# Other layouts for two DRAM scratch tensors, other places for an attention head's loads, and an own staging tile for the new frames' result

## The chip, the cores and the metric

The program runs on one core of a Trainium2 chip. A core has a matrix engine (TensorE, called PE in the profile; its weight loads are PEld), a vector engine (DVE), a scalar engine (ACT), a general engine (GpSimd, POOL) and a sync engine (SP). They run their own instruction streams side by side and wait for each other with semaphores. SP and POOL issue the transfers between on-chip memory (SBUF) and DRAM; 16 DMA engines carry them out. The metric is the device time of one execution in microseconds (us), the median of the runs.

## The reference, cut to what matters

One layer of a streaming encoder. 1024 prompt frames and 64 new frames of running streams, 1088 tokens of width 1024, go through the same weights:

```python
xn = rmsnorm(x)
cb, cc, ch, q, k, v, ga, gb = split(xn @ w_in)      # 512 x 6, 1024 x 2
cv = causal_conv(cc * ch)                           # width 3, per channel
ya = (cb * cv) @ w_conv_out
yb = band_attend(q, k, v, rel_bias) @ w_attn_out    # 8 heads of 64
x  = x + (sigmoid(ga) * ya + sigmoid(gb) * yb) @ w_out
x  = x + (silu(n @ w1) * (n @ w3)) @ w2             # n = rmsnorm(x)
y  = rmsnorm(x)
```

A frame attends to its own chunk of 64 and the 8 chunks before it; the new frames attend to 512 cached rows of k and v and to themselves. All of it is fp32.

## The kernel before, in words

**Numbers in two parts.** A factor of an fp32 product is held as a high and a low part, and a product is three matmuls: high by high, high by low, low by high. `split` (L120 to L123) makes the parts: an ACT copy to the high part (L122), then a DVE subtraction for the low one (L123).

**Stages.** By the times of the profiled execution: norm, transposes and the values v (0 to 120 us); the seven other products of the input projection (120 to 376.5), each in a scheme of seven half-size products per quarter; a first part of the gate products (from 376.5), attention with gate products between its steps (393.9 to 565.3), the rest of the gate products (565.3 to 598.5), then `ya` and `yb`, their merge, the output projection and the feed-forward products.

**The projection's results.** `put_v` (around L344) writes v, split, to the scratch tensor `v_d` in DRAM, 128 tokens at a time, each token a run of 128 numbers (64 high, 64 low). `cb_done` (L655) makes `u = cb * cv` a half row block at a time, splits it and stores both parts to `u_d`. Scratch tiles rotate through a few places.

**Gate products.** `gates` (L794) makes 16 of the gate products' row blocks in 32 pieces of 24 matmuls (128x272). A piece is added up in a PSUM bank, copied by DVE to a tile `gst` (two places), and stored by POOL to `ga_d` or `gb_d`. `BEHIND` pieces come after attention, 16 (`WITH`) are spread between attention's steps, and 32 - 16 - `BEHIND` come ahead of it: 11, 16 and 5 before the change.

**Attention.** `attention` (L1011) runs 8 heads of 9 steps; step 8 is the new frames. In each turn PE makes the scores of one step, transposes the probabilities of the step two turns back, multiplies an earlier pair of steps with the values (four turns back, five for step 8), and fills in gate matmuls. `pin` (L770) fixes the order of these on PE, DVE and ACT. The first matmul of step 0 reads `qd` and `kd`. `head_load` (L846) loads a head's queries (`qd`), keys (`kd`), bias (`bb`), values (`vd`), and for step 8 the cached and new keys and values (`ksd`, `vsd`, one place each). It is called at step 3 of the head before. All these loads stand in SP's one queue, which issues in order, and an issue waits until its destination is free. A scheduler places instructions that aren't pinned, so the order in a queue isn't the order of the calls.

**combine** (L876). A result `pv` goes by an ACT copy to the tile `ca` (one place), POOL adds its two halves into `co` (three places, named `co_s` for the new frames) and stores it to `o_d`. For step 8 ACT also copies the rows of reciprocals to a tile `rows`, which POOL stores to `rc_d`.

**After attention.** SP loads the first gates, `u` (L1060, both parts, four transfers) and, for each of four row blocks k, `r`, `o2` and `rc` (L1064 to L1068); `r` has two places. DVE adds and multiplies them (L1071, L1072), and `split` writes `ob`. `ya` (L1079 on) multiplies `u`, `yb` multiplies `ob`, and L1088 to L1094 merge them with the gates.

Of the kernel before, what the change touches and what calls it, by code (L numbers as in the profile page):

```python
# [9 lines left out]
F32 = mybir.dt.float32  # L10
F32R = mybir.dt.float32r
# [5 lines left out]
P = 128  # L17
D = 1024
KD = D // P
TP = 1024  # L20
TS = 64
# [14 lines left out]
KB = [2, 3, 3, 3]  # L36
C_CB, C_CC, C_CH, C_Q, C_K, C_V, C_GA, C_GB = 0, 512, 1024, 1536, 2048, 2560, 3072, 4096
WITH = 16
BEHIND = 11


class Quarters:
# [23 lines left out]
def encoder_kernel(ctx: ExitStack, tc: tile.TileContext, ins, outs):  # L66
# [23 lines left out]
    h_d = dr.tile([NF // 2, 7, P, 4 * 2 * P], F32, name="h_d")  # L90
    hs_d = dr.tile([NF // 2, P, 2, 2 * TS], F32, name="hs_d")
    x21_d = dr.tile([P, 8, HT], F32, name="x21_d")
    u_d = dr.tile([4, P, 2, T], F32, name="u_d")

    q_d = dr.tile([NH, HD, 2, T], F32, name="q_d")
    k_d = dr.tile([NH, HD, 2, TK], F32, name="k_d")
    v_d = dr.tile([NH, TK, 2 * HD], F32, name="v_d")
    ga_d = dr.tile([D, T], F32, name="ga_d")
    gb_d = dr.tile([D, T], F32, name="gb_d")
    o_d = dr.tile([2, ATT, T], F32, name="o_d")  # L100
# [241 lines left out]
    def put_v(st, src, n, row, queue):  # L342
        st = st.bitcast(F32R).rearrange("p (h l d) -> p h l d", h=NH, l=2)
        s = src.rearrange("p (h d) -> p h d", h=NH)  # L344
        split(st[:n, :, 0, :], st[:n, :, 1, :], s[:n])
        queue.dma_start(
            v_d[:, row : row + n, :].rearrange("h t e -> t h e"),
            st[:n].rearrange("p h l d -> p h (l d)").bitcast(F32),
        )

# [202 lines left out]
    def stage():  # L553
        return slot(STAGE, 2 * HT).bitcast(F32R).rearrange("p (l n) -> p l n", l=2)
# [100 lines left out]
    def cb_done(u):  # L655
        def f(r, h, src, snap):
            s = summed(src, snap)
            for a, at, n in spans(h):
                vec.tensor_tensor(s[:, a : a + n], s[:, a : a + n], ccs[r][:, at : at + n], op=ALU.mult)
            st = stage()  # L660
            split(st[:, 0], st[:, 1], s)
            nc.sync.dma_start(u_d[2 * u + r, :, :, h * HT : (h + 1) * HT], st.bitcast(F32))

        return f

# [180 lines left out]
    def head_load(h):  # L846
        q = []
        for l in range(2):
            qq = hd_pool.tile([P, T], F32R, tag=f"q{l}", name=f"qd{h}_{l}")
            for j in range(2):  # L850
                nc.sync.dma_start(qq[j * HD : (j + 1) * HD].bitcast(F32), q_d[h, :, l])
            q.append(qq)
        k = hd_pool.tile([P, TP], F32R, tag="k", name=f"kd{h}")
        ks = hd_pool.tile([P, CACHE + TS], F32R, tag="ks", name=f"ksd{h}", bufs=1)
        v = hd_pool.tile([P, 8, P], F32R, tag="v", name=f"vd{h}")
        vs = hd_pool.tile([P, 5, P], F32R, tag="vs", name=f"vsd{h}", bufs=1)
        halves = [(slice(l * HD, (l + 1) * HD), k_d[h, :, l]) for l in range(2)]
        for e in range(2):
            for ls, src in halves:
                nc.sync.dma_start(k[ls, 512 * e : 512 * e + 512].bitcast(F32), src[:, 576 * e : 576 * e + 512])  # L860
        b = bb[:, h % 2]
        near = bias_d[h, 127 : 127 + P * 383].rearrange("(p n) -> p n", n=383)
        far = bias_rows(h, 0, 384)
        nc.sync.dma_start(b[:HD, 384:576], near[:HD, :192])
        nc.sync.dma_start(b[HD:, 384:], near[HD:, :256])
        nc.sync.dma_start(b[:HD, :384], far[:HD])
        nc.sync.dma_start(b[HD:, HD:384], far[HD:, HD:])
        nc.sync.dma_start(v.bitcast(F32), v_d[h, :TP].rearrange("(b p) e -> p b e", p=P))
        for ls, src in halves:
            nc.sync.dma_start(ks[ls, :CACHE].bitcast(F32), src[:, T:])  # L870
            nc.sync.dma_start(ks[ls, CACHE:].bitcast(F32), src[:, 512:576])
        nc.sync.dma_start(vs[:, :4].bitcast(F32), v_d[h, TP : TP + CACHE].rearrange("(b p) e -> p b e", p=P))
        nc.sync.dma_start(vs[:TS, 4].bitcast(F32), v_d[h, TP + CACHE :])
        heads[h] = (q, k, ks, v, vs, b)

    def combine(h, pv, n, tok, nm):  # L876


        def f():
            a = at_pool.tile([P, 2, 256], F32, tag="a", name=f"ca{nm}", bufs=1)  # L880
            o = at_pool.tile([P, 256], F32, tag="o", name=f"co{nm}", bufs=3)
            copy_at(a[:, :, :n], pv)
            pool_e.tensor_tensor(o[:, :n], a[:, 0, :n], a[:, 1, :n], op=ALU.add)
            to = o_d[:, h * HD : (h + 1) * HD]
# [86 lines left out]
    def values(h, t):  # L971
        q, k, ks, v, vs, bias = heads[h]
        pv = bank("pv", f"pv{h}_{t}").rearrange("p (a b) -> p a b", a=2)
        if t == 8:
# [3 lines left out]
                mm_at(pv[:, :, :TS], vs[:r, i, :], pt[:r, :, i, :], start=i == 0, stop=i == 4)  # L978
            tr = pv[:9, 1, P:]
            turned(tr, sums.pop(h), ident)  # L980
            rows = at_pool.tile([P, P], F32, tag="rows", name=f"rows{h}", bufs=1)[:9]

            def out():
                copy_at(rows, tr)
                for e in range(2):
                    nc.gpsimd.dma_start(
# [2 lines left out]
                    c = e * HT + 512  # L989
                    nc.gpsimd.dma_start(rc_d[h : h + 1, c : c + 32], rows[8:9, 32 * e : 32 * e + 32])  # L990

            todo["o"].append(out)
            combine(h, pv[:, :, :TS], TS, TP, f"{h}_s")
            return
        g = t // 2
        pt = pts.pop((h, g))
# [14 lines left out]
    def attention():  # L1011
# [7 lines left out]
        for i in range(n + 5):  # L1019
            target = first + upto[min(i, n + 3)]  # L1020
            gate((given[0] + target) // 2)
            if i < n:
                h, t = order[i]
                if t == 3 and h + 1 < NH:
                    head_load(h + 1)
                done.append(scores(h, t))
            for kind in ("gate", "hi", "o", "inv", "lo"):
                take(kind)
# [17 lines left out]
        return sg  # L1046

    head_load(0)

    nc.sync.dma_start(xn.t[0, 1].rearrange("p l k t -> p (l k) t").bitcast(F32), x21_d)  # L1050
    gate(24 * (4 * len(GATES) - WITH - BEHIND), False)
# [5 lines left out]
    mp = pg_stack.enter_context(tc.tile_pool(name="mgp", bufs=4, reuse_waits="tile"))  # L1057
    sg = gates_in(0)
    for k in range(4):
        nc.sync.dma_start(u.t[:, :, k].bitcast(F32), u_d[k])  # L1060
    for k in range(4):
        rc, o2 = (ob.t[:, l, k].bitcast(F32) for l in range(2))
        r = mp.tile([P, T], F32, tag="rc", name=f"r{k}", bufs=2)
# [596 lines left out]
```

## Time and profile before

| | |
|---|---|
| runs shown | 1533.78 us median, 1532.72 to 1537.23 (3 runs) |
| the profiled execution | 1538.47 us, span 1536.7 us |
| mean granted TensorE clock | 0.988 of full speed |
| busy | PE 96%, DVE 64%, ACT 44%, POOL 12% of the span |
| DRAM | 173.29 MB read, 94.15 MB written |
| packets of all transfers | 174110, 269.35 MB |

"Busy" is the share of the span in which an engine ran an instruction. "L779" is a line of the kernel; many instructions of attention carry L779, the line of the helper that pins them, and are told apart by their tiles. A "wait" row says which engine's instruction waited, and for whose. In a list of windows the columns are: window, its length, then busy time (and instructions) of PE, PEld, DVE, ACT and POOL, the granted clock of TensorE as a share of full speed, the share of time in which the 16 DMA engines were busy, and what they moved in GB/s.

### The profile page before, as it was taken

To read this page: it belongs to the slowest core of one execution; us is meant where nothing else is said; L and a number is where in the kernel's file an instruction comes from. 1 tells how busy PE (TensorE), PEld (TensorE's weight loads), DVE (VectorE), ACT (ScalarE), POOL (GpSimd) and SP (SyncE) were. 2 spreads that over 40 slices of the span, in tenths; PEclk is the share of its full clock that TensorE was granted. 3 is DMA by queue.
4 is the path that set the end of the run, shared out by engine and by line. 5 is a ranking of instruction groups with operands and counts; after the bars stand their busy time and mean duration, and the time that the engine had idled before them with its cause. 6 is when DMAs were issued, how large, how long until landed. Compare 5 with 4: busy or idle time off the path is not lost.

```text
span 1536.7 us, 26391 instructions
## 1 busy us (share of the span) xinstructions
PE 1476.1 (96%) x10130; PEld 1380.4 (90%) x10130; DVE 976.6 (64%) x1819; ACT 668.7 (44%) x1363; POOL 186.7 (12%) x308
## 2 busy tenths in 40 slices
PE   7999999999989998899999999999999999899997
PEld 5799999999878898898888999999999998688886
DVE  6886465463456643764379766666666668856577
ACT  6654333333467751453156444444444445503123
POOL 1210010000255551000000011000010111000000
PEclk9999999999999999999999999999999999999999
DMA  7596613226878977654432343333344449676675
GB/s 237 178 312 228 212 55 132 71 85 208 219 167 193 201 186 235 196 154 151 142 130 70 141 155 141 132 123 124 142 155 141 155 153 311 230 238 226 219 263 199
DMA packets 174110, 269.35 MB, mean 175 GB/s; under 512 B 25537, under 2 KB 107649, under 8 KB 173857
## 3 DMA queue, kind: packets, MB, share of 16 engines
q1 hardware_dynamic: 144624, 200.45, 41.8%
q0 software_dynamic: 28208, 65.12, 12.6%
q8 instruction: 80, 1.31, 0.4%
q10 hardware_dynamic: 1152, 2.10, 0.4%
q14 instruction: 46, 0.37, 0.1%
HBM read 173.29 MB, written 94.15 MB: 174 GB/s over the span
## 4 chain that ended last, share of the span: by engine, by line
PE 62%; issue 19%; DMA 11%; DVE 4%; ACT 2%; POOL 1%; SPq 0%; POOLq 0%; ACTq 0%; DVEq 0%
PE Ab L239 7%; PE Aa L239 7%; PE A L1577 7%; PE Db L239 4%; PE Da L239 4%; PE D L1577 3%; PE Bb L239 2%; PE B L1577 2%; PE g L779 2%; PE Ak L239 2%; DMA kd<-k_d 2%; PE Ba L239 2%; PE Acc L239 2%; PE Ach L239 2%; PE Acb L239 2%
## 5 line engine op out<-in xcount | busy, mean ns | idle before, releaser
L1577 PE MATMUL A<-ring,ht 128*128 128x512 f32 x528 | 126.7, 393 | 3.9 <-ACT acc L1587 2.2
L1577 PEld LDWEIGHTS A<-ring,ht 128*128 128x128 f32 x528 | 98.8, 188 | 27.5 <-ACT acc L1587 3.5
L779 PE MATMUL g<-xn,whp 128*128 128x272 f32 x512 | 105.7, 297 | 1.0 <-ACT scr L531 1.0
L1296 POOL DMA_DIRECT2D h_d<-hq x77 | 41.1, 533 | 418.5 <-DVE hq L123 242.8
L122 ACT CAST ring<-w2r 128x512 fp32r<-128x512 f32 (+1 forms) x78 | 43.4, 587 | 108.1 <-PE A L1577 52.4
L122 ACT CAST hq<-sa 128x512 fp32r<-128x512 f32 x77 | 47.7, 620 | 85.3 <-DVE sa L1308 56.6
L779 PEld LDWEIGHTS g<-xn,whp 128*128 128x128 f32 x512 | 82.5, 192 | 2.5 <-ACT scr L531 1.2
L779 PE MATMUL g<-xn,wlp 128*128 128x272 f32 x256 | 75.8, 296 | 0.0
L123 DVE TENSOR_TENSOR hq<-sa,hq 128x512 fp32r<-128x512 f32 x77 | 53.2, 691 | 32.6 <-ACT hq L122 32.4
L779 DVE CUSTOM_DVE_ANT_0 p<-s,bb 128x640 f32<-128x640 f32 (+5 forms) x72 | 47.9, 665 | 40.1 <-PE s L779 20.4
L1577 PE MATMUL D<-ring,ht 128*128 128x512 f32 x264 | 63.9, 393 | 2.4 <-ACT acc L1587 2.4
L123 DVE TENSOR_TENSOR wla<-rawa,wha 128x512 fp32r<-128x512 f32 x56 | 38.5, 688 | 40.5 <-ACT wha L122 40.5
L239 PE MATMUL Aa<-tt,wha 128*128 128x272 f32 x352 | 58.9, 288 | 3.8 <-ACT tt L122 2.5
L1577 PEld LDWEIGHTS D<-ring,ht 128*128 128x128 f32 x264 | 49.5, 188 | 14.2 <-ACT acc L1587 2.8
L302 PE MATMUL yb<-ob,whp 128*128 128x272 f32 x256 | 52.7, 302 | 8.8 <-ACT ob L122 6.2
L123 DVE TENSOR_TENSOR ring<-w2r,ring 128x512 fp32r<-128x512 f32 (+1 forms) x78 | 49.0, 647 | 16.0 <-ACT ring L122 15.7
L239 PE MATMUL Ab<-mg,whb 128*128 128x272 f32 x352 | 58.4, 288 | 0.0
L239 PE MATMUL Aa<-mg,wha 128*128 128x272 f32 x352 | 58.3, 288 | 0.0
L239 PE MATMUL Ab<-tt,whb 128*128 128x272 f32 x352 | 58.2, 287 | 0.0
L122 ACT CAST wha<-rawa 128x512 fp32r<-128x512 f32 x56 | 34.8, 622 | 51.2 <-PE Ab L239 35.3
L239 PEld LDWEIGHTS Aa<-tt,wha 128*128 128x128 f32 x352 | 49.6, 188 | 4.7 <-ACT tt L122 2.9
L779 ACT ACTIVATE p<-p,mx 128x640 f32<-128x640 f32 (+5 forms) x72 | 50.9, 707 | 3.9 <-DVE mx L779 3.2
(540 smaller groups left out, 4331.7 us busy)
## 6 DMA issues: line engine op xcount, KB each, us to landing
h_d<-hq POOLq DMA_DIRECT2D x77, 512.0 KB, 3.5
ht<-h_d SPq DMA_DIRECT2D x154, 256.0 KB, 3.6
rawa<-in_w_ff SPq DMA_DIRECT2D x11, 1024.0 KB, 5.6
rawb<-in_w_ff SPq DMA_DIRECT2D x11, 1024.0 KB, 5.3
w2r<-in_w_ff SPq DMA_DIRECT2D x11, 1024.0 KB, 5.8
qd<-q_d SPq DMA_DIRECT2D x32, 272.0 KB, 7.6
u_d<-scr SPq DMA_DIRECT2D x8, 544.0 KB, 3.8
ga<-ga_d SPq DMA_DIRECT2D x32, 136.0 KB, 2.7
```

The costliest lines, as they stand in the source:

```text
L122: act.copy(hi, src)
L123: vec.tensor_tensor(lo, src, hi.bitcast(F32), op=ALU.subtract)
L239: mm(t[:, j, :HN], w[:, k, :], x[p][:, l, k, j * HN : (j + 1) * HN], start=p in (1, 2, 7) and k == 0 and n == 0, stop=k == 3 and n == 2, s ...
L302: mm(out, l, r, start=k + j == 0, stop=k == kt - 1 and j == 2)
L779: return lambda *a, **kw: pin(f(*a, **kw))
L1296: nc.gpsimd.dma_start(h_d[p, c - 1], hq.rearrange("p i l t -> p (i l t)").bitcast(F32))
L1577: mm(t, ht[k][:, j, x], w[:, l], start=p in (1, 2, 7) and k == 0 and n == 0, stop=k == len(ks) - 1 and n == 2, skip_group_check=p in (6, 5 ...
```

## The change

1. `u_d` holds `u` unsplit. `cb_done` stores the product as it is, and after attention `u` is loaded into the place of its low part and split there.
2. `v_d` is laid out by partition: for a head and a partition, the 13 blocks of tokens follow each other. A head's load of `vd` is one run of 4096 bytes in each partition in place of 8 runs of 512, that of `vsd` one of 2048 in place of 4 of 512. The stores keep runs of 512 bytes.
3. A head's loads are called in two lots: `head_load` at step 1 of the head before, `frames_load` (`ksd`, `vsd`) at step 5.
4. The new frames' `ca` has a tile of its own (`a64`), and the rows of reciprocals go to an unused corner of `co_s` in place of a tile of their own.
5. `BEHIND` is 10: the gate products are 6 pieces ahead of attention, 16 in it and 10 behind.

```diff
-BEHIND = 11
+BEHIND = 10
...
-    u_d = dr.tile([4, P, 2, T], F32, name="u_d")
+    u_d = dr.tile([4, P, T], F32, name="u_d")
...
-    v_d = dr.tile([NH, TK, 2 * HD], F32, name="v_d")
+    v_d = dr.tile([NH, P, (TK + P - 1) // P, 2 * HD], F32, name="v_d")
...
-            v_d[:, row : row + n, :].rearrange("h t e -> t h e"),
+            v_d[:, :n, row // P].rearrange("h t e -> t h e"),
...
-            st = stage()
-            split(st[:, 0], st[:, 1], s)
-            nc.sync.dma_start(u_d[2 * u + r, :, :, h * HT : (h + 1) * HT], st.bitcast(F32))
+            nc.sync.dma_start(u_d[2 * u + r, :, h * HT : (h + 1) * HT], s)
...
-        nc.sync.dma_start(v.bitcast(F32), v_d[h, :TP].rearrange("(b p) e -> p b e", p=P))
-        for ls, src in halves:
+        nc.sync.dma_start(v.bitcast(F32), v_d[h, :, :8])
+        heads[h] = [q, k, None, v, None, b]
+
+    def frames_load(h):
+
+        ks = hd_pool.tile([P, CACHE + TS], F32R, tag="ks", name=f"ksd{h}", bufs=1)
+        vs = hd_pool.tile([P, 5, P], F32R, tag="vs", name=f"vsd{h}", bufs=1)
+        for l in range(2):
+            ls, src = slice(l * HD, (l + 1) * HD), k_d[h, :, l]
             nc.sync.dma_start(ks[ls, :CACHE].bitcast(F32), src[:, T:])
             nc.sync.dma_start(ks[ls, CACHE:].bitcast(F32), src[:, 512:576])
-        nc.sync.dma_start(vs[:, :4].bitcast(F32), v_d[h, TP : TP + CACHE].rearrange("(b p) e -> p b e", p=P))
-        nc.sync.dma_start(vs[:TS, 4].bitcast(F32), v_d[h, TP + CACHE :])
-        heads[h] = (q, k, ks, v, vs, b)
-
-    def combine(h, pv, n, tok, nm):
+        nc.sync.dma_start(vs[:, :4].bitcast(F32), v_d[h, :, 8:12])
+        nc.sync.dma_start(vs[:TS, 4].bitcast(F32), v_d[h, :TS, 12])
+        heads[h][2], heads[h][4] = ks, vs
+
+    def combine(h, pv, n, tok, nm, more=None):
...
-            a = at_pool.tile([P, 2, 256], F32, tag="a", name=f"ca{nm}", bufs=1)
+            w = 256 if tok < TP else TS
+            a = at_pool.tile([P, 2, w], F32, tag=f"a{w}", name=f"ca{nm}", bufs=1)
             o = at_pool.tile([P, 256], F32, tag="o", name=f"co{nm}", bufs=3)
+            if more:
+                more(o)
             copy_at(a[:, :, :n], pv)
...
-            rows = at_pool.tile([P, P], F32, tag="rows", name=f"rows{h}", bufs=1)[:9]
-
-            def out():
+
+            def out(o):
+                rows = o[:9, P:]
                 copy_at(rows, tr)
...
-            todo["o"].append(out)
-            combine(h, pv[:, :, :TS], TS, TP, f"{h}_s")
+            combine(h, pv[:, :, :TS], TS, TP, f"{h}_s", out)
...
-                if t == 3 and h + 1 < NH:
+                if t == 1 and h + 1 < NH:
                     head_load(h + 1)
+                elif t == 5 and h + 1 < NH:
+                    frames_load(h + 1)
...
     head_load(0)
+    frames_load(0)
...
     for k in range(4):
-        nc.sync.dma_start(u.t[:, :, k].bitcast(F32), u_d[k])
+        f = u.t[:, 1, k].bitcast(F32)
+        nc.sync.dma_start(f, u_d[k])
+        split(u.t[:, 0, k], u.t[:, 1, k], f)
```

**SP's queue where a head's loads stand.** A row is a transfer: its line, destination, source and shape; numbers in names tell tiles apart. Before:

```order
L870 DMA ksd_4764<-k_d 64x512
L871 DMA ksd_4764<-k_d 64x64
L851 DMA qd_0_5033<-q_d 64x1088 x2
L851 DMA qd_1_5036<-q_d 64x1088
L872 DMA vsd_4766<-v_d 128x4x128
L873 DMA vsd_4766<-v_d 64x128
L851 DMA qd_1_5036<-q_d 64x1088
L860 DMA kd_5039<-k_d 64x512 x4
L864 DMA bb<-bias_d 64x192
```

The same place with the change:

```order
L873 DMA ksd_4833<-k_d 64x512
L874 DMA ksd_4833<-k_d 64x64
L849 DMA qd_0_4987<-q_d 64x1088 x2
L849 DMA qd_1_4990<-q_d 64x1088
L875 DMA vsd_4834<-v_d 128x512
L876 DMA vsd_4834<-v_d 64x128
L849 DMA qd_1_4990<-q_d 64x1088
L856 DMA kd_4993<-k_d 64x512 x4
L860 DMA bb<-bias_d 64x192
```

Nothing moved: a head's `vsd` still stands ahead of the next head's `kd`. Only the shape of the `vsd` transfer differs.

**DVE after attention**, where the copies of the last gate pieces (`gst`), the additions and multiplications of `r` and the splits stand. Before:

```order
L779 COPY gst_0_6756<-g_0_6731 128x272
L779 COPY gst_1_6784<-g_1_6759 128x272
L1071 TENSOR_TENSOR r_6485<-r_6485,ob 128x1088
L779 COPY gst_2_6812<-g_2_6787 128x272
L1072 TENSOR_TENSOR r_6485<-r_6485,ob 128x1088
L779 COPY gst_3_6840<-g_3_6815 128x272
L123 TENSOR_TENSOR ob<-r_6485,ob 128x1088
```

The same place with the change:

```order
L777 COPY gst_1_6650<-g_1_6625 128x272
L123 TENSOR_TENSOR u<-u 128x1088
L777 COPY gst_2_6678<-g_2_6653 128x272
L123 TENSOR_TENSOR u<-u 128x1088 x2
L777 COPY gst_3_6706<-g_3_6681 128x272
L123 TENSOR_TENSOR u<-u 128x1088
L777 COPY gst_0_6740<-g_0_6715 128x272
L1081 TENSOR_TENSOR r_6497<-r_6497,ob 128x1088
L777 COPY gst_1_6768<-g_1_6743 128x272
L1082 TENSOR_TENSOR r_6497<-r_6497,ob 128x1088
L123 TENSOR_TENSOR ob<-r_6497,ob 128x1088
```

The four subtractions of `u` stand between the copies of the 26th to 29th of the 32 pieces, and the first addition of `r` has moved from behind the 30th copy to behind the 29th.

**PE ahead of the first scores**, `s_0`; `g` are the gate pieces. Before:

```order
L779 MATMUL g_2_4136<-xn_96,wlp_4_3821 128x272
L779 MATMUL g_3_4164<-xn_95,whp_0_3816 128x272 x2
L779 MATMUL g_3_4164<-xn_95,wlp_0_3817 128x272
L779 MATMUL s_0_4171<-kd_4004,qd_0_3998 128x128
L779 MATMUL s_0_4171<-kd_4004,qd_1_4001 128x128
```

The same place with the change:

```order
L777 MATMUL g_3_4148<-xn_96,wlp_4_3805 128x272
L777 MATMUL g_2_4176<-xn_95,whp_0_3859 128x272 x2
L777 MATMUL g_2_4176<-xn_95,wlp_0_3860 128x272
L777 MATMUL s_0_4183<-kd_3988,qd_0_3982 128x128
L777 MATMUL s_0_4183<-kd_3988,qd_1_3985 128x128
```

One whole gate piece more stands ahead of the first scores.

More of the change, by code (lines that the diff above doesn't have):

```diff
@@ L853, in head_load @@
         k = hd_pool.tile([P, TP], F32R, tag="k", name=f"kd{h}")
-        ks = hd_pool.tile([P, CACHE + TS], F32R, tag="ks", name=f"ksd{h}", bufs=1)
         v = hd_pool.tile([P, 8, P], F32R, tag="v", name=f"vd{h}")
-        vs = hd_pool.tile([P, 5, P], F32R, tag="vs", name=f"vsd{h}", bufs=1)
         halves = [(slice(l * HD, (l + 1) * HD), k_d[h, :, l]) for l in range(2)]
```

## The prediction

> **What bounds the kernel now.** I read the page's busy shares first, then the execution cut into its stages, then PE's waits in the stages that the change touches.
>
> ```profile
> PE 1476.1 (96%) x10130; PEld 1380.4 (90%) x10130; DVE 976.6 (64%) x1819; ACT 668.7 (44%) x1363; POOL 186.7 (12%) x308
> 120.00:376.50 256.50, 256.47 (x2054) 255.65 (x2053) 141.99 (x224) 96.73 (x175) 7.79 (x15) 1.00 0.40 133
> 376.50:393.90 17.40, 16.43 (x130) 16.07 (x128) 2.13 (x5) 1.13 (x2) 1.65 (x3) 1.00 0.98 309
> 393.90:565.30 171.40, 155.76 (x1076) 143.41 (x1075) 103.87 (x260) 116.03 (x281) 87.89 (x130) 0.96 0.80 184
> 565.30:598.50 33.20, 33.20 (x265) 33.20 (x266) 4.29 (x9) 5.50 (x13) 8.51 (x15) 1.00 0.96 286
> 598.50:628.10 29.60, 19.74 (x111) 17.59 (x110) 20.02 (x25) 6.48 (x8) 2.17 (x4) 0.79 0.57 173
> ```
>
> PE bounds the whole. A saving off PE is worth something only where PE stands idle or at a lower clock: 171.40 - 155.76 = 15.6 us in attention, and 29.60 - 19.74 = 9.9 us behind the last gate product, where the clock is 0.79. In the projection (120 to 376.5) PE is busy 256.47 of 256.50 us, so nothing taken from other engines there shows. Where the idle time goes is told by PE's waits from 376.5 to 628.1 (total, count, longest):
>
> ```profile
> PE s L779 <- DMA kd<-k_d: 8.9, 6, 1.9
> PE yb L302 <- ACT ob L122: 6.2, 4, 3.6
> PE t L779 <- DVE mx L779: 2.7, 2, 2.3
> PE yb L302 <- DVE ob L123: 1.5, 2, 0.9
> PE ya L302 <- DVE gst L779: 1.1, 1, 1.1
> PE yb L302 <- DVE ga L1088: 1.0, 1, 1.0
> ```
>
> In attention most of it is one thing: step 0 of a head waits for its keys. Behind attention it is `yb` waiting for `ob`. The first two windows of the next view, two stretches at the start of attention, show that short waits cost twice, since PE runs at half its clock after them; the other two lie in the middle of attention.
>
> ```profile
> 397.00:400.00 3.00, 3.00 (x16) 3.00 (x15) 1.33 (x5) 0.61 (x1) 0.00 (x0) 0.50 0.94 264
> 404.70:407.00 2.30, 2.30 (x11) 2.26 (x10) 1.12 (x3) 1.12 (x3) 0.00 (x0) 0.50 1.03 269
> 436.00:455.00 19.00, 16.67 (x109) 15.24 (x109) 9.41 (x27) 11.17 (x28) 7.78 (x13) 0.91 0.77 188
> 474.00:495.00 21.00, 19.12 (x127) 17.60 (x128) 12.72 (x33) 14.07 (x36) 10.73 (x18) 0.92 0.95 195
> ```
>
> **Part 1, the projection: 0.** `cb_done` loses 8 casts and 8 subtractions and half of what it stores. Their prices stand in the groups by line:
>
> ```profile
> L123 DVE TENSOR_TENSOR scr<-scr 128x544 fp32r<-128x544 f32 (+1 forms) x20 | 14.4, 718 | 9.0 <-ACT scr L122 8.6
> L122 ACT CAST scr<-scr 128x544 fp32r<-128x544 f32 (+1 forms) x20 | 12.8, 642 | 19.3 <-DVE scr L659 12.3 <-DMA v_d<-scr 3.1 <-DVE scr L533 2.3
> ```
>
> That is 8 x 0.72 = 5.7 us of DVE and 8 x 0.64 = 5.1 us of ACT, hidden behind a PE that is never idle; without that cover it would be up to 10.8 us. A loss is excluded nearly as well: the store now reads the tile that the sum was made in, so that tile comes free only when the store has landed, but PE's 0.03 us of idle time leaves room for a late tile.
>
> **Part 2, the start of attention: -3.3 us.** One gate piece moves from behind attention to ahead of it. The two rows are the first scores and a row of the chain of waits:
>
> ```profile
> 395.85 0.42 PE L779 MATMUL s<-kd,qd 128*128 128x128 f32 x2 [1.87 <-DMA kd<-k_d]
> 374.69 10.57 DMA ga_d<-scr
> 385.28 10.44 DMA kd<-k_d
> 396.27 2.36 PE g L779 x13
> ```
>
> The keys land at 395.85 whatever PE does; they are issued as soon as a store of the projection has landed. A piece of 24 matmuls takes 11 pieces in 33.20 us, so 3.02 us. It covers the 1.87 us whole. The halved clock that follows (3.00 us at 0.50) loses 1.5 us; I take 1.4, as a second wait at 402, for the exponential, may stay and have its own 2.30 us at 0.50. Sum 3.3, between 1.9 (the clock falls anyway) and 5. The piece itself is neither gained nor lost: what is added here is taken away behind attention.
>
> A rule speaks against the term for the clock. The Trainium skill, in "TensorE: Matmul & The Clock Gate", section "What's actually happening", lets the clock fall only after an idle window of some 3.4 us, free-running; by it a wait of 1.87 us would cost no clock and the term would be 1.9. The rows above, with 0.50 behind the wait of 1.87 us, do not agree with that figure, and I go by the rows.
>
> **Part 3, heads 1 to 7: -6 us.** First what does not happen. The loads are called two steps sooner, but SP's queue reads row for row as before: a head's `vsd` stands ahead of the next head's `kd`, and waits for its only place, which the `pv` of the head before gives back. So "sooner" is worth 0 here. What changes is how long the transfers take.
>
> ```profile
> SPq L872 <- DMA vd<-v_d: 10.0, 3, 4.4
> q1 hardware_dynamic: 24439, 24.43, 60.5%
> vd<-v_d SPq DMA_DIRECT2D x8, 512.0 KB, 8.3
> kd<-k_d SPq DMA_DIRECT2D x28, 128.0 KB, 6.9
> vsd<-v_d SPq DMA_DIRECT2D x8, 256.0 KB, 6.9
> ...
> q1 hardware_dynamic: 2485, 8.21, 82.0%
> ```
>
> The two rows of queue q1 are of attention (171.5 us) and of the stretch behind it (33.2 us). They give a price by size: 0.605 x 16 x 171.5 / 24439 = 68 ns for a packet of 1000 bytes, 0.82 x 16 x 33.2 / 2485 = 175 ns for one of 3304. A straight line through both is 21 ns and 0.0466 ns a byte, an estimate: 45 ns for 512 bytes, 117 for 2048, 212 for 4096. So `vd` falls from 1024 x 45 = 46 to 128 x 212 = 27 us of one engine, `vsd` from 512 x 45 = 23 to 128 x 117 = 15: together 27 / 16 = 1.7 us of all 16, in a head of 21.4 us that keeps them busy for 0.80 x 21.4 = 17.1. A tenth of the traffic goes. The keys' 6.9 us to landing lose a tenth, 0.7; and SP's 10.0 us of waiting for `vd` ahead of `vsd`, which delay the keys behind it in three heads, lose some 0.5 each, 0.2 a head. So the keys come 0.9 us sooner. Five waits of heads 1 to 7 hold 8.9 - 1.9 = 7.0, and one of 1.8 is booked to `wlp`: 6 x 0.9 = 5.4, all inside waits of 1.5 on average. Of the clock lost in the two middle stretches (0.09 x 19.0 + 0.08 x 21.0 = 3.4 us) I give back a fifth, 0.6. Sum 6. The bounds: 0, if landing is latency and not traffic; 12, if all of the 8.8 and the 3.4 goes.
>
> By the Trainium skill, "DMA: Bandwidth & Descriptors", section "Specifications", 512 bytes already run at line rate, and then longer runs gain nothing: the term would be 0. That is the second way below; the two rows of q1, 68 ns for 1000 bytes and 175 for 3304, speak against it, though no row isolates 512 from 4096 bytes.
>
> **The own place for `pv`: 0.** ACT waited 6.2 us in seven times for POOL's `co_s` before `ca`:
>
> ```profile
> ACT ca L779 <- POOL co_s L883: 6.2, 7, 1.8
> o_d<-co POOLq DMA_DIRECT2D x32, 128.0 KB, 7.4
> ```
>
> That goes, but PE's row of waits has no `pv` or bank that `ca` sets free, so it is idle time of ACT. The rows of reciprocals now wait for the stores from a `co` place, three results back; 40 results in 171.4 us are 4.3 us apart, so 12.9 us back, and the stores land in 7.4: the new wait is empty. If it were not, `ca`, the exponentials and with them PE would queue behind it.
>
> **Part 4, behind attention: -6 us.** The chain there, in order of time, SP, DVE and PE:
>
> ```profile
> 565.40 3.30 SPq L1060 DMA_DIRECT2D u<-u_d  x4
> 599.47 0.44 DVE L779 COPY gst<-g 128x272 f32<-128x272 f32 x1 [4.66 <-DMA gb_d<-gst]
> 602.64 1.28 DVE L1071 TENSOR_TENSOR r<-r,ob 128x1088 f32<-128x1088 f32 x1
> 607.96 0.33 SPq L1064 DMA_DIRECT2D r<-o_d  x1
> 624.75 1.92 PE L302 MATMUL yb<-ob,whp 128*128 128x272 f32 x5 [3.61 <-ACT ob L122]
> L1071 DVE TENSOR_TENSOR r<-r,ob x4: 1282/1284/1285, 602.6 to 619.7; 128x1088 f32<-128x1088 f32 x4
> L123 DVE TENSOR_TENSOR ob<-r,ob x4: 1291/1293/1293, 606.6 to 624.7; 128x1088 fp32r<-128x1088 f32 x4
> u<-u_d SPq DMA_DIRECT2D x4, 1088.0 KB, 15.2
> gb_d<-gst POOLq DMA_DIRECT2D x8, 136.0 KB, 7.4
> ```
>
> The transfers are at 0.96 of the time from 565.3 on. The first addition of `r` starts 37.3 us after 565.3, behind `gst` copies that each wait for a store through the same engines (7.4 us, two places). From there the chain runs by itself: the third `r` is loaded when the first is split (607.96), and the last part of `ob` comes 22 us after the first addition. The change takes 4 x 544 KB = 2.2 MB off; at the window's 286 GB/s that is 7.6 us. From the other side: the first addition now stands behind the 29th copy, whose piece leaves PE 7 x 3.02 = 21.1 us after attention; with 7.4 us for a store that is 28.5, or 8.8 sooner. I take 7.6. PE reaches `ya` 3.0 us sooner than before, as one piece has moved, so the waits shrink by 7.6 - 3.0 = 4.6 of 9.9 us. The clock at 0.79 loses 0.21 x 19.7 = 4.1 us; a third of it comes back with the shorter waits, 1.4. Sum 6.0.
>
> What is added there: four casts and four subtractions of 128x1088, by the rows of `r` 1.29 us each on DVE, 5.2 in all (ACT, idle 27 of 33 us, has room). DVE is busy 4.29 of 33.20 us there, so it fits, as long as `u` has landed. Each subtraction waits for its load and its cast; queued behind it are the `gst` copies 27 to 29 and the first `r`, for which POOL's stores and `yb` wait. Bounds: 13, all waits and most of the clock; -8.2, if the 5.2 and the piece's 3.0 both count in full.
>
> **Sum.** 3.3 + 6 + 6 = 15.3 us off the profiled 1538.5: 1523.2. The median of the runs lies 4.7 lower than that execution, so 1518.5, said as 1519.
>
> **The rivals**, on the median.
>
> *The keys' waits stay.* For it: SP's queue is unchanged and a landing of 6.9 us has a fixed share. Against it: transfers at 0.80 of the time. Gain 3.3 + 6.0 = 9.3: 1524.5.
>
> *The chain behind attention keeps its pace.* For it: `gst` has two places still, and a store's time may be latency. Against it: 0.96 and 286 GB/s. Gain 3.3 + 6: 1524.5. Both together: 3.3, so 1530.5.
>
> *`u` in the way, and slower.* The four subtractions of `u` hold up the `gst` copies, as a load of 15.2 us lands late, and the first addition of `r` slips by their 5.2 us while PE comes 3.0 us sooner: 8.2 more of waiting, less 3.3 at the start, and nothing in the heads: 4.9 more, 1538.7. It decides once the first addition starts later than 42 us after attention's last `pv` (37.3 + 5.2), and is against a load of half the bytes.
>
> *Everything goes.* Idle 15.6 + 9.9 and the 4.1 of clock behind attention: 29.6 off, 1504.2. Against it: the waits for exponentials and maxima are not touched.
>
> **How the numbers follow.** The forecast 0.40; the keys' waits stay 0.17; the chain keeps its pace 0.15; both 0.13; `u` in the way 0.10; everything 0.05. The range 1507 to 1532 leaves out the last two, 0.15; the forecast's own is 1513 to 1523. A difference of under 0.3%, 4.6 us, cannot be told from none: faster is below 1529.2, slower above 1538.4. Faster 0.40 + 0.17 + 0.15 + 0.05 = 0.77, no change 0.13, slower 0.10.
>
> **What would show it.** Packets fall from 174110 by 8 x 896 for `vd`, 8 x 384 for `vsd` and some 1500 for `u`, to about 162300. The first `s` has no wait for `kd`. The keys' waits of heads 1 to 7 sum to 2 to 4 us, and `vd` and `vsd` land sooner; if they land sooner and the keys don't, part 3 is wrong. The first `r` starts about 29 to 30 us after the last `pv`, and `yb`'s waits halve; if it starts at 37, the bytes of `u` were not what held it. The projection keeps its 256.5 us; if it grows, part 1 is wrong.

## The result, and the profile after

| | before | the change |
|---|---|---|
| median of 17 runs each | 1536.95 us (1530.16 to 1541.78) | 1524.02 us (1515.17 to 1532.82) |
| the profiled execution | 1538.47 us | 1515.17 us |
| ratio | | 0.9916, 95% interval 0.9899 to 0.9932 |

The change is faster by 12.9 us (10.5 to 15.5 by the interval). The forecast was 1519, with 15.3 us won. The profiled execution of the change is the fastest of its runs and 8.9 us below their median, so a difference of the two profiles shows more than the change is worth. A second profile, e7 below, lies nearer.

The page's line of packets, and the stages, for the changed kernel (columns as before; the last row reaches as far behind the gate products as the waits do):

```profile
DMA packets 162334, 264.90 MB, mean 175 GB/s; under 512 B 25536, under 2 KB 95360, under 8 KB 162080
120.00:376.50 256.50, 256.47 (x2053) 255.65 (x2052) 136.83 (x217) 92.00 (x167) 7.78 (x15) 1.00 0.38 125
376.50:396.80 20.30, 19.27 (x153) 19.05 (x152) 3.50 (x7) 2.36 (x4) 2.73 (x5) 1.00 0.94 288
396.80:555.30 158.50, 149.30 (x1075) 138.24 (x1073) 102.44 (x258) 115.34 (x280) 87.56 (x129) 1.00 0.83 196
555.30:585.60 30.30, 30.30 (x242) 30.23 (x243) 11.83 (x16) 10.13 (x18) 9.03 (x16) 1.00 0.78 252
585.60:610.50 24.90, 17.48 (x115) 16.06 (x114) 17.72 (x24) 6.58 (x10) 1.08 (x2) 0.90 0.65 189
```

The packets are 162334, as worked out. The projection keeps its 256.47 us of PE, with DVE 5.2 and ACT 4.7 us less busy under it. Attention's window is 12.9 us shorter than before. Two things have changed in it: idle time, from 15.6 to 9.2 us, and PE's busy time for as many matmuls, from 155.76 to 149.30, because the clock is 1.00 in place of 0.96. Behind attention the transfers stand at 0.78 in place of 0.96.

PE's waits from 376 to 640, and the chain behind attention (`r` and `u` by their tiles):

```profile
PE s L777 <- DMA kd<-k_d: 6.4, 5, 2.3
PE yb L302 <- ACT ob L122: 5.6, 2, 5.2
PE t L777 <- DVE mx L777: 1.4, 3, 0.5
PE yb L302 <- DVE ob L123: 1.2, 2, 0.7
...
L1081 DVE TENSOR_TENSOR r<-r,ob x4: 1280/1288/1293, 582.2 to 601.0; 128x1088 f32<-128x1088 f32 x4
...
L123 DVE TENSOR_TENSOR ob<-r,ob x4: 1291/1292/1293, 586.2 to 606.3; 128x1088 fp32r<-128x1088 f32 x4
...
L1069 SPq DMA_DIRECT2D u<-u_d x4: 430/464/862, 555.7 to 557.1; - x4
L123 DVE TENSOR_TENSOR u<-u x4: 1280/1280/1283, 569.0 to 577.5; 128x1088 fp32r<-128x1088 f32 x4
...
DMA to landing us min/median/max: 7.5/9.4/11.0
```

The first scores have no wait left. `u` lands 9.4 us after its issue (15.2 before), its subtractions are over at 578.8, and the first addition of `r` starts at 582.2, 27.1 us after the last `pv` (37.6 before, counted from the same instruction at 565.0). The rows of waits shrank less: those for keys from 8.9 us, of which 7.0 stand in heads 1 to 7, to 6.4, and those of `yb` for `ob` from 7.7 to 6.8.

### The profile page after: what moved, and what is told of

Read it like the earlier page. It is cut to its first block, busy times and chain, and to the rows that moved or that the text cites. A ratio compares the mean times of both kernels' runs of the same rounds, so it can differ in the third digit from the quotient of the medians.

```text
span 1513.4 us, 26409 instructions
## 1 busy us (share of the span) xinstructions
PE 1464.5 (97%) x10130; PEld 1371.1 (91%) x10130; DVE 974.9 (64%) x1815; ACT 669.0 (44%) x1359; POOL 186.7 (12%) x308
## 2 busy tenths in 40 slices
DMA packets 162334, 264.90 MB, mean 175 GB/s; under 512 B 25536, under 2 KB 95360, under 8 KB 162080
## 4 chain that ended last, share of the span: by engine, by line
PE 63%; issue 20%; DMA 8%; DVE 4%; ACT 1%; SPq 1%; POOL 1%; POOLq 0%; DVEq 0%; ACTq 0%
PE Ab L239 8%; PE Aa L239 8%; PE A L1587 7%; PE Db L239 4%; PE Da L239 4%; PE D L1587 3%; PE Bb L239 2%; PE B L1587 2%; PE g L777 2%; PE Ba L239 2%; DMA kd<-k_d 2%; PE Ak L239 2%; PE Acc L239 2%; PE Ach L239 2%; PE Acb L239 2%
## 5 line engine op out<-in xcount | busy, mean ns | idle before, releaser
L123 DVE TENSOR_TENSOR ring<-w2r,ring 128x512 fp32r<-128x512 f32 (+1 forms) x78 | 49.1, 646 | 12.0 <-ACT ring L122 11.8
```

The lines of the kernel that those rows point to most:

```text
L123: vec.tensor_tensor(lo, src, hi.bitcast(F32), op=ALU.subtract)
```

## The experiments

All times are against the kernel before on the same chip. The profiles differ by some us in places that no edit touches. The first gate product, for one, starts at 377.87 us in the profile of the kernel before and, in e1, which is the same program up to there, at:

```profile
383.51 0.51 PE L779 MATMUL g<-xn,whp 128*128 128x272 f32 x2 [0.97 <-ACT scr L531]
```

So the table takes stretches that begin and end inside the part in question. "Attention" is from the first scores to the last `pv`, with PE's busy time in it; "heads" is the part of PE's idle time that lies just before the first scores of heads 1 to 7; "behind" is from the first product of `ya` to the first of the output projection; "`r`" is the start of its first addition after the last `pv`.

| kernel | won, us (95% interval) | attention | PE busy | heads | `r` | behind |
|---|---|---|---|---|---|---|
| before | 0 | 169.2 | 155.4 | 8.9 | 37.6 | 113.3 |
| e1 piece | -0.9 (-3.1 to 1.4) | 162.2 | 149.5 | 10.1 | 36.3 | 117.8 |
| e2 u | 5.1 (2.9 to 7.2) | 167.8 | 152.6 | 10.5 | 27.3 | 107.3 |
| e3 v | 3.2 (1.1 to 5.4) | 160.7 | 150.6 | 7.6 | 38.3 | 114.0 |
| e4 own place | -0.5 (-2.8 to 1.8) | 167.3 | 153.3 | 11.6 | 34.5 | 110.5 |
| e5 piece and u | 6.0 (3.1 to 8.9) | 165.9 | 151.9 | 10.2 | 26.5 | 108.9 |
| e6 all but the piece | 10.6 (7.5 to 13.7) | 161.5 | 152.1 | 6.4 | 28.8 | 110.4 |
| e9 all but v | 9.1 (6.1 to 11.8) | 164.8 | 152.0 | 9.5 | 28.7 | 110.1 |
| e10 all but u | 4.5 (1.8 to 7.1) | 161.5 | 150.7 | 7.9 | 36.9 | 118.1 |
| e11 all but own place | 13.8 (9.7 to 18.0) | 156.7 | 149.8 | 5.6 | 26.6 | 107.1 |
| the change, first profile | 12.9 (10.5 to 15.5) | 158.3 | 149.1 | 6.4 | 27.1 | 108.0 |
| e7 the change again | 12.9 (10.5 to 15.4) | 160.4 | 150.5 | 7.2 | 27.0 | 107.0 |
| e8 two places for vsd | 21.2 (18.8 to 23.8) | 154.6 | 148.7 | 0.0 | 28.2 | 109.0 |
| e12 as e8, pieces behind | 19.2 (15.2 to 23.4) | 152.0 | 145.4 | 3.5 | 27.7 | 105.2 |

e12 has 14 of 16 pieces in attention, so its busy time there isn't to be compared with the others.

**e1, the piece alone.**

```diff
-BEHIND = 11
+BEHIND = 10
```

> The kernel before with BEHIND = 10 alone. The prediction's account: 3.3 us won at the start of attention, up to 3.0 lost behind it because the chain of r still ends when it did, so 0 to 3.3 us faster (ratio 0.998 to 1.000), no wait for kd before the first scores, and yb's waits for ob longer by about 3 us. Rival (the piece carries much of the gain): 5 us or more faster (ratio under 0.997), because the first heads never fall to half the clock.

Ratio 1.0006 (0.9991 to 1.0020). No wait is left at the first scores, 4.5 us appear behind, and `yb`'s waits for `ob` are 11.4 us in place of 7.7: the prediction's account holds.

**e2, u alone.**

```diff
...
-            split(st[:, 0], st[:, 1], s)
-            nc.sync.dma_start(u_d[2 * u + r, :, :, h * HT : (h + 1) * HT], st.bitcast(F32))
+            nc.sync.dma_start(u_d[2 * u + r, :, h * HT : (h + 1) * HT], s)
...
-        nc.sync.dma_start(u.t[:, :, k].bitcast(F32), u_d[k])
...
+        nc.sync.dma_start(f, u_d[k])
+        split(u.t[:, 0, k], u.t[:, 1, k], f)
```

> The kernel before with u stored in one part and split after its load, nothing else. The prediction's account: the bytes hold up the first addition of r, which starts about 30 us after attention's last pv in place of 37; with no piece moved all of that counts, so 7.6 us of waiting and about 2 of clock, 6 to 10 us faster (ratio 0.9935 to 0.996). Rival (a store's latency paces the gst copies and with them r): first addition at 35 to 37, 0 to 2 us faster. Rival (u in the way): slower by up to 5.

Ratio 0.9967 (0.9953 to 0.9981). The first addition of `r` starts 27.3 us after the last `pv` in place of 37.6, and `u` isn't in the way. DVE around that addition, in the kernel before and then in e2:

```profile
594.36 0.44 DVE L779 COPY gst<-g 128x272 f32<-128x272 f32 x1 [3.79 <-DMA gb_d<-gst]
...
602.28 0.44 DVE L779 COPY gst<-g 128x272 f32<-128x272 f32 x1 [2.37 <-DMA gb_d<-gst]
602.64 1.28 DVE L1071 TENSOR_TENSOR r<-r,ob 128x1088 f32<-128x1088 f32 x1
```

```profile
594.53 0.44 DVE L777 COPY gst<-g 128x272 f32<-128x272 f32 x1 [2.46 <-DMA gb_d<-gst]
594.89 1.28 DVE L1071 TENSOR_TENSOR r<-r,ob 128x1088 f32<-128x1088 f32 x1
```

The copies at 594.36 and 594.53 are the seventh after attention in each kernel, 29.4 and 26.9 us after the last `pv`. In e2 the addition stands right behind it, in the kernel before behind the ninth. So of the 10.3 us, some 2.4 are copies that wait less for their stores, and some 8 are the addition's place in DVE's order. Its two operands had landed 24.2 and 27.3 us after the last `pv` in the kernel before, ahead of the seventh copy already. In every profile with `u` in two parts the addition stands behind the ninth copy, in every profile with `u` in one part behind the seventh. The loads behind it come sooner as well (the second operand lands at 19.7 in place of 27.3), but no run has fewer bytes with the old order, so the bytes alone aren't shown to be the cause. PE's waits for `ob` in e2:

```profile
PE yb L302 <- ACT ob L122: 1.3, 1, 1.3
...
PE yb L302 <- DVE ob L123: 0.7, 2, 0.4
```

They fell from 7.7 us to 2.0, while the clock behind attention is about as low as before (0.95 and 0.94). The gain, 5.1 us, is a little under the 6 to 10 that were expected. With 11 pieces behind attention these waits have only 2.0 us left to lose.

**e3, v's layout alone.**

```diff
-    v_d = dr.tile([NH, TK, 2 * HD], F32, name="v_d")
+    v_d = dr.tile([NH, P, (TK + P - 1) // P, 2 * HD], F32, name="v_d")
...
```

> The kernel before with v_d laid out by partition, nothing else; the order of all instructions is the one before. The prediction's account: vd lands in about 7 us in place of 8.3, vsd in about 6 in place of 6.9, the keys' waits of heads 1 to 7 shrink from 8.8 to about 3.4, 6 us faster (ratio 0.996). Rival (512 bytes already run at the full rate, or landing is latency): vd and vsd land as before, 0 to 1 us faster.

Ratio 0.9979 (0.9965 to 0.9993), between the two. What the layout saves on the DMA engines is read from SP's queue in attention, the kernel before (395.85 to 565.0) and then e3 (396.0 to 556.7):

```profile
q1 hardware_dynamic: 24203, 24.18, 60.9%
vd<-v_d SPq DMA_DIRECT2D x8, 512.0 KB, 8.3
kd<-k_d SPq DMA_DIRECT2D x28, 128.0 KB, 6.9
vsd<-v_d SPq DMA_DIRECT2D x8, 256.0 KB, 6.9
```

```profile
q1 hardware_dynamic: 13920, 24.14, 61.8%
vd<-v_d SPq DMA_DIRECT2D x8, 512.0 KB, 8.2
kd<-k_d SPq DMA_DIRECT2D x28, 128.0 KB, 6.3
vsd<-v_d SPq DMA_DIRECT2D x8, 256.0 KB, 6.8
```

0.609 x 169.15 = 103.0 us of 16 engines became 0.618 x 160.7 = 99.3. That is 3.7 us for 10283 packets fewer, 5.8 ns a packet or 0.46 us a head, where the prediction had 1.7. In these two profiles `vd` and `vsd` land as late as before, as the rival had it, and the keys 0.6 us sooner. More profiles say otherwise for `vd`. The medians to landing in attention lie, for the six profiles with the old layout (before, e1, e2, e4, e5, e9) and the six with the new (e3, e6, e7, e10, e11 and the first of the change), at 8.1 to 9.1 and 7.5 to 8.2 us for `vd`, 6.6 to 7.4 and 6.1 to 6.9 for `vsd`, and 6.5 to 7.2 and 5.9 to 6.7 for `kd`. The waits follow: in the column "heads" the old layout has 8.9 to 11.6 us, the new one 5.6 to 7.9, 3.3 less on average, about what the kernel won. By the Trainium skill, "DMA: Bandwidth & Descriptors", section "Why small descriptors are slow (HBM only)", a packet has a small fixed cost on top of its bytes; the 5.8 ns agree with that in kind.

**e4, the own place alone.**

```diff
...
-            a = at_pool.tile([P, 2, 256], F32, tag="a", name=f"ca{nm}", bufs=1)
...
+            a = at_pool.tile([P, 2, w], F32, tag=f"a{w}", name=f"ca{nm}", bufs=1)
...
```

> The kernel before with a tile of its own for the new frames' ca and the rows of reciprocals in co_s, nothing else. The prediction's account: ACT's wait of 6.2 us for POOL's co_s goes and PE has no row that waits for it, so no difference (ratio 0.999 to 1.001). Rival (ACT's queue is what the start of a head waits for): the casts and exponentials behind ca come up to 0.9 us sooner in seven heads, 3 to 6 us faster (ratio 0.996 to 0.998).

Ratio 1.0003 (0.9988 to 1.0018): nothing, as predicted. The calls of the loads in two lots have no run of their own. In the profiles before and after, SP issues its loads in the same order from 330 us on until far behind attention, so they leave that queue's order as it was.

The four parts alone add up to about 7 us, the change gives 12.9. By the five intervals the surplus of 6 has some 5 us either way, an estimate, so it is only just clear of the scatter. The next runs look for it.

**e5, piece and u**, the edits of e1 and e2 together:

```diff
-BEHIND = 11
+BEHIND = 10
...
+        split(u.t[:, 0, k], u.t[:, 1, k], f)
```

> The kernel before with u in one part and BEHIND = 10, and neither v's layout nor the own place. The four parts alone add up to 7.4 us, the change gives 12.9. Theory A (the piece and u need each other: the piece moved ahead covers the wait at the start, but its place behind attention is only free once u's bytes are gone): 8 to 10 us faster (ratio 0.9935 to 0.995), yb's waits below those of the kernel before. Theory B (the surplus comes from v's layout with the own place, inside attention): the sum of the two alone, 4 to 5 us faster (ratio about 0.997).

Ratio 0.9961 (0.9942 to 0.9980), 6.0 us: between theories A and B, and too wide to tell them apart. `yb`'s waits for `ob` are 8.5 us, not below the 7.7 of the kernel before, as theory A would have them.

**e6, the change without the piece.**

```diff
-BEHIND = 10
+BEHIND = 11
```

> The changed kernel with BEHIND = 11. Theory A: the sum of the parts alone, 8 us faster than before (ratio 0.9948). Theory B: 11 us or more (ratio 0.993 or less), nearly the whole change. In both the first scores wait again, about 1.5 us.

Ratio 0.9931 (0.9911 to 0.9951), 10.6 us, nearer to B. The piece is worth some 2 us in company. The time alone doesn't settle it; the stretches in the table do better, with e10.

**e10, the change without u in one part.**

```diff
...
-            nc.sync.dma_start(u_d[2 * u + r, :, h * HT : (h + 1) * HT], s)
...
+            split(st[:, 0], st[:, 1], s)
+            nc.sync.dma_start(u_d[2 * u + r, :, :, h * HT : (h + 1) * HT], st.bitcast(F32))
...
-        split(u.t[:, 0, k], u.t[:, 1, k], f)
+        nc.sync.dma_start(u.t[:, :, k].bitcast(F32), u_d[k])
```

> The changed kernel with u stored in two parts. The profiles so far say that a piece fewer behind attention is paid there in full while u's bytes are in the way: from the first product of ya to the first of the output projection 117 us, as with the piece alone, in place of 107 to 108. Then the change loses 8 to 10 us of its 13 and is 3 to 5 faster than before (ratio 0.997 to 0.998). Rival (u is worth what it was alone, 5 us): 8 us faster than before (ratio 0.995).

Ratio 0.9971 (0.9954 to 0.9988): 4.5 us are left, so `u` is worth 8.4 in company and 5.1 alone, which differ by less than their intervals. The stretch behind attention, for the kernel before, e1 and e10:

```profile
598.50:711.80 113.30, 102.84 (x770) 100.46 (x768) 77.29 (x171) 48.84 (x124) 2.17 (x4) 0.94 0.53 161
```

```profile
595.30:713.10 117.80, 103.26 (x771) 100.32 (x769) 76.92 (x172) 48.25 (x124) 2.17 (x4) 0.94 0.53 157
```

```profile
588.90:707.00 118.10, 105.05 (x770) 102.70 (x769) 76.93 (x170) 48.53 (x124) 2.16 (x4) 0.91 0.53 158
```

With `u` in two parts it is 110.5 to 114.0 us long with 11 pieces behind attention (before, e3, e4) and 117.8 and 118.1 with 10. With `u` in one part it is 107.3 and 110.4 with 11 (e2, e6) and 107.0 to 110.1 with 10 (the change, e5, e7, e9, e11). So a piece fewer costs 5 us behind attention while `u` is stored in two parts and `r` comes late, and nothing once `u` is in one part. That is theory A's mechanism, seen in at least two profiles of each of the four kinds. The times bear it out only loosely: in e5 the piece and `u` are worth 1.8 us more together than apart, so where the rest of the surplus of 6 us comes from is not shown.

**e9, the change without v's layout.**

```diff
-    v_d = dr.tile([NH, P, (TK + P - 1) // P, 2 * HD], F32, name="v_d")
+    v_d = dr.tile([NH, TK, 2 * HD], F32, name="v_d")
...
```

> The changed kernel with v_d in the layout before. The prediction's account: its 6 us go, 7 us faster than before are left (ratio 0.9955), and from the first scores to attention's last pv it takes 6 to 7 us longer than the changed kernel's 159, as the profiles with that layout did. Rival (the single run's 3 us is all that v is worth): 10 us faster than before (ratio 0.9935).

Ratio 0.9941 (0.9923 to 0.9960), 9.1 us: the layout is worth 3.8 us in company, 3.2 alone, nearer to the rival's 3 than to the 6 of the prediction. Attention is 164.8 us long, in the five other profiles with the old layout 162.2 to 169.2, and with the new one 156.7 to 161.5 in six. On average that is 6.3 us, of which 4.3 are idle time and 2.0 PE's busy time. The medians give 3 to 4; single profiles scatter by that much.

**e11, the change without the own place.**

```diff
...
-            a = at_pool.tile([P, 2, w], F32, tag=f"a{w}", name=f"ca{nm}", bufs=1)
+            a = at_pool.tile([P, 2, 256], F32, tag="a", name=f"ca{nm}", bufs=1)
...
```

> The changed kernel without the own tile for the new frames' ca and with the rows of reciprocals in their own tile. If it is worth nothing in company too: as the changed kernel, 12 to 14 us faster than before (ratio 0.991 to 0.992). Rival (the surplus of the whole over its parts sits here): 8 to 9 us faster than before (ratio 0.9945).

Ratio 0.9910 (0.9883 to 0.9937): worth nothing in company either.

**e7, the change again**, without an edit.

> The changed kernel again, unaltered, for a second profile: the first lies at the lower end of its runs. 12 to 14 us faster than before (ratio 0.991 to 0.992). From the first gate product to the first product of the output projection about 320 us, more than the 316 of the first profile; part of the difference shown by the two profiles lies ahead of the first gate product.

Ratio 0.9916 (0.9900 to 0.9932). From the first gate product (380.13) to the first of the output projection (697.1) it takes 317.0 us, a little under the 320 expected, against 333.9 before and 315.9 in the first profile. Its attention and the stretch behind it:

```profile
399.10:559.50 160.40, 150.49 (x1074) 139.36 (x1072) 102.52 (x258) 114.78 (x279) 87.11 (x130) 0.99 0.84 194
590.10:697.10 107.00, 99.88 (x771) 98.26 (x769) 74.09 (x168) 48.38 (x124) 1.08 (x2) 0.97 0.57 167
```

**e8, two places for vsd**, on the changed kernel. The keys still came late, and the row of SP's queue that can explain it, `vsd` ahead of the next head's `kd`, had not moved.

```diff
-        vs = hd_pool.tile([P, 5, P], F32R, tag="vs", name=f"vsd{h}", bufs=1)
+        vs = hd_pool.tile([P, 5, P], F32R, tag="vs", name=f"vsd{h}")
...
-        s = at_pool.tile([P, 640], F32, tag="s", name=f"p{h}_{t}", bufs=4)
+        s = at_pool.tile([P, 640], F32, tag="s", name=f"p{h}_{t}", bufs=3)
```

> The changed kernel with two places for vsd (and three in place of four for the probabilities, to make room), so that SP's queue issues vsd before the next head's qd and kd and nothing in it waits for the pv of the head before. Theory P (the keys are late because SP's queue holds them behind vsd): kd is issued 5 us or more sooner, the keys' waits of 6.4 us fall below 2, another 5 to 8 us faster than the change (ratio to before 0.987 to 0.989). Rival (the transfers are saturated at 0.83 of the time in attention, a sooner issue only queues longer): within 2 us of the change. Rival (the third place for the probabilities was needed): slower than the change.

Ratio to before 0.9862 (0.9845 to 0.9878): 21.2 us, 8.3 more than the change. SP's longest waits among a head's loads, in e7 and then in e8 (L875 issues `vsd`, L873 `ksd`), for e8 the keys' time to landing, and its attention:

```profile
SPq L875 <- PE pv L777: 15.8, 6, 5.9
```

```profile
SPq L873 <- PE s L777: 5.2, 2, 3.5
...
kd<-k_d SPq DMA_DIRECT2D x29, 128.0 KB, 7.4
```

```profile
402.50:557.10 154.60, 148.74 (x1074) 138.01 (x1073) 103.15 (x258) 113.44 (x279) 86.92 (x129) 1.00 0.84 201
```

No wait for `kd` is left on PE, although a key takes longer to land than before (7.4 us). From the keys' issue to a head's first scores there are 9.0 to 14.4 us in heads 2 to 7, against 5.8 to 9.3 in e7: 2.8 more on average, less than the 5 expected, and enough. So the theory holds: what kept the keys late was their place in SP's queue, behind a transfer that waits for the head before.

The profile shows less than the medians, as e8's profiled execution is the slowest of its five runs: attention is 5.8 us shorter than in e7, and the stretch behind it 2.0 longer. PE's other idle time in attention is 5.8 us in place of 2.7, so 3.1 of the 7.2 us came back as other waits. Whether the third place for the probabilities has a part in that isn't shown.

**e12, more pieces behind**, on e8.

```diff
-WITH = 16
-BEHIND = 10
+WITH = 14
+BEHIND = 12
```

> The kernel with two places for vsd, and of the 16 gate pieces in attention two moved behind it (14 and 12). The waits of yb for ob there were 6.4 and 1.4 us, and two pieces take 6.0, so they fall below 2. Theory P (in attention PE no longer waits for keys, and the two pieces there were plain work): 4 to 6 us faster than with 16 and 10, ratio to before 0.982 to 0.984. Rival (in attention the pieces fill the time in which PE waits for exponentials and casts): attention keeps its length, so 6 us are added behind it and 5 won, no difference.

Ratio to before 0.9875 (0.9848 to 0.9901), which can't be told from e8's. Its attention, the gate products behind it, and the rest:

```profile
396.40:548.40 152.00, 145.38 (x1027) 133.73 (x1025) 101.50 (x256) 113.13 (x280) 86.34 (x128) 0.99 0.86 200
548.40:585.00 36.60, 36.60 (x291) 36.52 (x291) 17.00 (x23) 11.31 (x20) 10.09 (x18) 1.00 0.78 244
585.00:690.20 105.20, 99.19 (x771) 97.92 (x769) 72.12 (x169) 48.11 (x125) 1.08 (x2) 0.98 0.55 165
```

The three stretches sum to 293.8 us and to 294.1 in e8. Two pieces are 6.0 us. Attention lost only 2.6 of them, and the 3.4 that stayed eat the 3.8 won behind. Of the 3.4, 1.7 are one stretch at half the clock that e8 doesn't have (from 485.6), and 0.8 are more idle time: PE now waits 3.4 us for the bias `bb` ahead of first scores. The rest isn't placed. The rival was right about the time; that the pieces had filled time in which PE waits anyway is shown in part only. By the medians e8 is the fastest kernel here.

## Why the prediction was right, point by point

**The sum**: 15.3 us were forecast, 12.9 measured, inside the range. By the gain the forecast is nearer than its one-sided rivals with 9.3, which lie outside the interval. The median itself, 1524.0, stands a little outside the forecast's own 1513 to 1523 and next to the 1524.5 of those rivals, since the kernel before came out 3.2 us above the three runs shown ahead. e9, without the layout, won 9.1 us where parts 2 and 4 together had 9.3; so by the medians the miss sits in part 3.

**Part 1, the projection, 0**: right, with its busy time to the hundredth.

**Part 2, the start, 3.3**: right in kind. The wait is gone: the first scores come 18.97 us after the first gate product in place of 17.98, so 2.0 us of the piece's 3.02 are won there. The clock was well guessed too: in the five profiles with 11 pieces behind attention it fell there for 2, 1, 0, 1 and 1 stretches of 3.4 us, each of which costs 1.7, so 1.7 us on average where 1.4 were taken. In the eight with 10 pieces it never fell there. By the times the piece's worth in company is 2.3 us (12.9 - 10.6), with some 4 us either way, so 3.3 isn't refuted.

**Part 3, the heads, 6**: the term of the sum that was mis-sized; 3.2 us alone and 3.8 in company. The way was the predicted one: the loads land sooner, and PE waits less for a head's keys. But the keys come 0.6 us sooner on average, where 0.9 were taken, and the waits of heads 1 to 7 lose 3.3 us, where 5.4 were; the named waits for keys sum to 6.4 and 7.2 us where 2 to 4 were forecast. The step that failed is the straight line through two rows of queue q1, which put 21 ns on every packet. Measured, a packet fewer saves 5.8 ns. The two rows were of different transfers in different stretches, and their slope took all of the difference for size. The keys' landing still fell by 0.6 of 6.9 us, nearly the tenth that was read from this price. As far as these runs show that is luck, since the transfers' time on the engines fell by only 3.7 us of 103.0. That "sooner" does nothing here was right, and so was its reason; e8 takes that reason away and wins 8.3 us. The rival "the keys' waits stay" was wrong by a third: 10.1 us became 6.8 on average.

The clock gave some of it as well. In attention it fell for 4, 0, 2, 3, 2 and 2 stretches of 3.4 us in the six profiles with the old layout, and for 0, 1, 2, 1, 1 and 0 in the six with the new. No run holds the waits and changes the clock, so how much of the layout's gain that is stays open. A single pair can mislead here: from before to e7 it looks like 4.9 us of clock and 3.9 of idle time, because the profile of the kernel before has the most such stretches of all.

**Part 4, behind attention, 6**: the sum was right, its steps only in part. `r` starts 10.5 us sooner (7.6 and 8.8 were the two estimates), and the stretch behind is 5.3 and 6.3 us shorter in the two profiles. But the step that was taken, fewer bytes and so faster stores and copies, gave the smaller part: the seventh copy after attention comes 2.6 us sooner, and the rest is the addition's place behind the seventh copy in place of the ninth (e2). The other estimate had seen that place, and both came to the same size; that is luck. Of e7's 6.3, 3.0 are clock (PE busy 102.84 to 99.88) and 3.3 waits, where 1.4 and 4.6 were taken, and `yb`'s waits for `ob` did not halve: they went from 7.7 to 6.8 us in both profiles. One thing was said too simply: that PE comes 3.0 us sooner was taken off as a fixed price. It is no price when the chain is early enough and 5 us when it isn't.

**The own place, 0**: right, alone and in company.

## What to carry to other kernels

A load that is called sooner isn't issued sooner while its queue holds an earlier entry that waits: look for the entry ahead of it, and give that one its second place (8.3 us here by the medians). Moving covering work away from a wait is free or costs its full length and more, depending on whether the chain behind that wait has been shortened first; test such edits together, not alone. A price per packet needs two kernels that move the same bytes in different packets; two stretches of one trace don't give it. Before a smaller transfer is called the cause of an earlier instruction, look whether that instruction's place in its engine's order has moved too.

## What the runs showed of the hardware

A short wait of PE can cost a fixed 1.7 us more. These are the stretches at the lower clock: four in attention and two behind it in the kernel before, then one behind it in the change.

```profile
397.00:400.40 3.40, 3.40 (x17) 3.32 (x15) 1.50 (x6) 0.95 (x2) 0.00 (x0) 0.50 0.94 258
403.80:407.20 3.40, 3.40 (x15) 3.06 (x14) 1.23 (x4) 1.12 (x3) 0.00 (x0) 0.50 1.02 278
441.20:444.60 3.40, 3.40 (x14) 2.91 (x12) 1.67 (x8) 1.12 (x5) 0.00 (x0) 0.52 0.83 205
478.90:482.30 3.40, 3.40 (x16) 2.88 (x14) 1.54 (x6) 1.47 (x4) 0.82 (x2) 0.50 0.87 234
608.60:615.30 6.70, 5.15 (x21) 4.83 (x22) 5.62 (x8) 1.10 (x1) 0.00 (x0) 0.50 0.92 259
622.20:629.00 6.80, 4.20 (x17) 3.88 (x18) 5.56 (x10) 3.87 (x8) 0.00 (x0) 0.50 0.32 99
```

```profile
605.60:612.30 6.70, 5.92 (x24) 5.60 (x25) 5.99 (x14) 4.20 (x10) 0.00 (x0) 0.50 0.18 49
```

Each is 3.4 us long, or twice that, at half the clock, so attention loses 1.7 us for each. PE's busy time in attention goes by such steps: 148.7 to 149.8 us with none (four profiles), 150.5 to 150.7 with one (three), 151.9 to 152.6 with two (four), 153.3 with three (e4), 155.4 with four (before).

Whether a wait costs these 1.7 us depends on where it lies. In all 14 traces the clock changes on one grid of 3.41 us that runs on through the execution. Four steps of that grid, each at full clock, two of the kernel before and then two of the change:

```profile
475.49:478.90 3.41, 1.56 (x12) 1.32 (x11) 1.67 (x4) 1.60 (x5) 1.39 (x3) 1.00 0.82 165
533.51:536.92 3.41, 1.70 (x15) 1.51 (x14) 2.29 (x5) 2.37 (x6) 2.69 (x4) 1.00 1.07 145
```

```profile
465.72:469.13 3.41, 2.67 (x21) 2.40 (x19) 3.05 (x7) 3.19 (x7) 2.16 (x4) 1.00 1.08 189
469.13:472.54 3.41, 1.81 (x12) 1.66 (x13) 0.00 (x0) 0.69 (x1) 0.81 (x1) 1.00 0.89 187
```

In the first PE is idle for 1.85 us, and the next step is at half the clock (478.90 above). In the second it is idle for 1.71, and the clock stays. In the change a longer wait, 2.35 us for keys until 470.73, lies across the border of two steps, 0.74 and 1.60 us, and costs nothing; so does one of 2.17 until 435.53 in e7. Counted over the steps at full clock from 376 to 700 us in all traces, the clock fell after each of the 27 with more than 1.85 us of idle time, after 10 of the 25 with 1.60 to 1.85, and after none of the 1213 with less. The grid lies differently to the program in each execution, so the same wait costs 1.7 us in one and nothing in another, and some of a run's scatter comes from that. The Trainium skill, "TensorE: Matmul & The Clock Gate", section "What's actually happening", tells of a free-running window of 3.4 us. The lengths agree with it, and so do starts 6.8, 37.4 and 37.7 us apart, which are 2, 11 and 11 windows. It lets the clock fall after a window of idle time; here half a window was enough.
